# Replacing a bitonic sort of 262,144 edge keys by a fitted network of shrinking gaps, row rotations and a transposed tail

## The chip, the cores and the metric

The kernel runs on one core of a Trainium2 chip. The metric is device time in microseconds of one launch. The engines that matter are TensorE (PE, with its weight loads as PEld), VectorE (DVE), ScalarE (ACT) and GpSimd (POOL); SyncE (SP) issues most DMAs.

## The reference

```python
N, E, D = 4096, 262144, 256
self_out = nodes @ w_self
src_feat = nodes[edges_src]
msg = src_feat @ w_msg
agg = np.zeros((N, D), dtype=np.float32)
np.add.at(agg, edges_dst, msg)
return (self_out + agg).astype(np.float32)
```

Every edge adds one transformed row to its destination. The edges are random, but the draw is the same each time.

## The kernel before

**Products.** The nodes are loaded by POOL's queue with a cast to bf16 (`nodes_bf`), written back to DRAM and read by SP as 64 transposing DMAs into `XT` (L203). TensorE forms `Y = nodes @ w_msg` in 64 products `y_ps` (L213), two for each of 32 blocks of nodes; ScalarE copies them to `Y` (L217).

**Keys.** The edges lie as 128 rows of 2048. Each becomes one whole number below 2^24, held in fp32: the lowest 7 bits are the source within its block of 128 nodes; the rest orders the edges by destination segment (10 segments of 384 nodes and one of 256), then by source block, then by destination. One segment with one source block is a *run*; there are 352.

**Sort.** A bitonic sort of all keys. `cpass` (L574) is one pass: two exchanges on VectorE (L582), a minimum and a maximum over half of the 2048 columns each. 66 passes sort the rows. Then 7 stages join the rows: `_switch` (L554) transposes 16 blocks of 128 x 128 through TensorE (L560) into PSUM, and ScalarE copies them back to SBUF (L563), so that distances between rows become distances between columns. The first and the last pass beside a switch are cut in four (`split=4`), so that a quarter can go on.

**Hand-over.** The sorted keys are cut into 2048 *chunks* of 128. `k16` is each chunk's least key (L225), `gi` that without its 7 low bits, the chunk's base. `gi` goes to DRAM and comes back to all partitions (`gball`, L251, L252), to be subtracted (`rel_b`, L310); small steps turn `gi` into an address in PSUM for each chunk (`poff`), which goes through DRAM into one row (`poffs`, L283).

**Counting and applying.** For every 32 chunks VectorE makes one-hots (L326): `e_oh` of the source in its block (128 wide) and `d_oh` of the destination counted from the chunk's base (W = 96 wide). A matmul for each chunk (L360, `count_mm`) adds e^T d to a ring of 6 PSUM banks, at the address that TensorE loads from `poffs`. Before a run its bank's edges are cleared (L360 too, with `zer`); after it ScalarE evicts the counts to `at` (L386), and TensorE multiplies them with the run's block of `Y` (L410, L415) into `out_ps`; L403 adds the self term at the head of a segment. Six chunks belong to a run (four in the last segment), 192 to a segment. The order of this part is written out by hand, and evictions, clears and applies stand at fixed chunks, so the bases have to lie within margins of the plan.

**Check.** A flag counts the chunks whose base lies outside the margins, or whose span may leave the window. If it isn't zero, `_any_edges` redoes the whole work edge by edge, in 2048 rounds.

The lines that decide how the sort is paced:

```python
for t, op in ((0, ALU.min), (1, ALU.max)):
    nc.vector.tensor_tensor(
        out=d4[:, :, t, :], in0=s4[:, :, 0, :], in1=hi, op=op
    )
```

The functions that the change touches:

Of the kernel before, what the change touches and what calls it, by code (L numbers as in the profile page):

```python
# [9 lines left out]
P = 128  # L10
FP32 = mybir.dt.float32
BF16 = mybir.dt.bfloat16
I32 = mybir.dt.int32
I64 = mybir.dt.int64
# [7 lines left out]
W = 96  # L22
# [6 lines left out]
MARG2 = 6  # L29
LAG = 12  # L30
PSUM0 = 0x2000000
SENT = float((1 << 24) - 1)
# [13 lines left out]
def kernel(  # L46
# [17 lines left out]
    NSTAGE = 18  # L64
    JBITS = 11
# [9 lines left out]
    gd = dram.tile([1, NCOL], FP32, name="gd")  # L75
    pd = dram.tile([1, NCOL], I32, name="pd")
    fd = dram.tile([1, P], FP32, name="fd")
# [9 lines left out]

    sgi = const.tile([P, 8], I32, name="sgi")
    sgx = const.tile([P, 8], I32, name="sgx")
    sgn = const.tile([P, 8], FP32, name="sgn")  # L90
    ksg = const.tile([P, 5], FP32, name="ksg")
    nc.gpsimd.iota(sgi[:], pattern=[[0, 8]], base=0, channel_multiplier=1)
    tss = nc.vector.tensor_single_scalar
    tt = nc.vector.tensor_tensor
    tss(out=sgx[:], in_=sgi[:], scalar=1, op=ALU.logical_shift_right)
    tt(out=sgx[:], in0=sgx[:], in1=sgi[:], op=ALU.bitwise_xor)
    for k in range(7):
        nc.vector.tensor_scalar(
            out=sgx[:, k:k + 1], in0=sgx[:, k:k + 1], scalar1=k, scalar2=1,
            op0=ALU.logical_shift_right, op1=ALU.bitwise_and,  # L100
        )
    tss(out=sgx[:, 7:8], in_=sgi[:, 7:8], scalar=1, op=ALU.bitwise_and)
    nc.vector.tensor_scalar(
        out=sgn[:], in0=sgx[:], scalar1=-2.0, scalar2=1.0, op0=ALU.mult, op1=ALU.add
    )
    for i, m in enumerate((1.0, 128.0, float((SW * (NB - 1)) << 7), float((SW << 7) - P), float(-(1 << 14)))):
        nc.vector.tensor_scalar(
            out=ksg[:, i:i + 1], in0=sgn[:, 7:8], scalar1=m, scalar2=None, op0=ALU.mult
        )

    sortp = tc.alloc_tile_pool(name="sortp", bufs=1)
    XA = [sortp.tile([P, NCOL], FP32, name=f"XA{i}") for i in range(2)]
    XB = [sortp.tile([P, NCOL], FP32, name=f"XB{i}") for i in range(2)]
    sids = [sortp.tile([P, P], FP32, name=f"sid{k}") for k in range(7)]
    for k in range(7):
        nc.gpsimd.tensor_scalar(
            out=sids[k][:], in0=ident[:], scalar1=sgn[:, k:k + 1], scalar2=None, op0=ALU.mult
        )
# [3 lines left out]
    for h in range(2):  # L122
        d64 = ldp.tile([P, HC], I64, name=f"d64_{h}")
        s64 = ldp.tile([P, HC], I64, name=f"s64_{h}")
        nc.sync.dma_start(
            d64[:], edges_dst.rearrange("(p j) -> p j", p=P)[:, h * HC:(h + 1) * HC]
        )
        nc.scalar.dma_start(
            s64[:], edges_src.rearrange("(p j) -> p j", p=P)[:, h * HC:(h + 1) * HC]
        )  # L130
        dlo = d64[:].bitcast(I32)[:, 0::2]
        slo = s64[:].bitcast(I32)[:, 0::2]
        hi = XB[h][:].bitcast(I32)
        seg = hi[:, 0:HC]
        blk = hi[:, HC:2 * HC]
        key = XA[0][:, h * HC:(h + 1) * HC]
        cut = XA[1][:, h * HC:(h + 1) * HC]
        nc.scalar.activation(out=key, in_=slo, func=ACTF.Copy, scale=ksg[:, 0:1])
        tss(out=blk, in_=slo, scalar=7, op=ALU.logical_shift_right)
        tss(out=seg, in_=dlo, scalar=7, op=ALU.logical_shift_right)  # L140
        nc.vector.scalar_tensor_tensor(
            out=cut, in0=seg, scalar=29.5, in1=blk, op0=ALU.is_gt, op1=ALU.mult
        )
        tss(out=seg, in_=seg, scalar=43, op=ALU.mult)
        tss(out=seg, in_=seg, scalar=7, op=ALU.logical_shift_right)
        for v, i in ((dlo, 1), (cut, 4), (seg, 2), (blk, 3)):
            nc.vector.scalar_tensor_tensor(  # L147
                out=key, in0=v, scalar=ksg[:, i:i + 1], in1=key, op0=ALU.mult, op1=ALU.add
            )
# [7 lines left out]
    jrow = const.tile([P, P, 2], BF16, name="jrow")  # L157
    lo_c = const.tile([P, G16], I32, name="lo_c")
    hi_c = const.tile([P, G16], I32, name="hi_c")
    lom_c = const.tile([P, G16], I32, name="lom_c")  # L160

# [58 lines left out]
    lane = _run_sort(nc, psum_sort, XA, XB, ident, sids, NSTAGE, JBITS)  # L220
    srt = XA[0]
    k16 = meta.tile([P, G16], FP32, name="k16")
    for q in range(4):
        _switch(nc, psum_sort, lane, srt, ident, q)
        nc.vector.tensor_reduce(  # L225
            out=k16[:, 4 * q:4 * q + 4],
            in_=_view3(srt[:, q * 512:(q + 1) * 512], P), axis=AX.X, op=ALU.min,
        )


# [5 lines left out]
    gi = meta.tile([P, G16], I32, name="gi")  # L236
    gn = meta.tile([P, G16], I32, name="gn")
# [3 lines left out]
    gb = meta.tile([P, G16], FP32, name="gb")  # L241
# [3 lines left out]
    gball = meta.tile([P, NCOL], FP32, name="gball")  # L245
    poffs = meta.tile([1, NCOL], I32, name="poffs")

    nc.vector.tensor_copy(out=k16i[:], in_=k16[:])
    tss(out=gi[:], in_=k16i[:], scalar=7, op=ALU.logical_shift_right)
    nc.vector.tensor_copy(out=gb[:], in_=gi[:])  # L250
    nc.sync.dma_start(gd[0, :].rearrange("(p g) -> p g", g=G16), gb[:])  # L251
    nc.sync.dma_start(gball[:], gd[0:1, :].broadcast_to([P, NCOL]))  # L252
# [8 lines left out]
    nc.vector.scalar_tensor_tensor(  # L261
        out=dl[:], in0=qa[:], scalar=float(-SW), in1=gi[:], op0=ALU.mult, op1=ALU.add
    )
    nc.vector.scalar_tensor_tensor(
        out=dl[:], in0=qb[:], scalar=-256.0, in1=dl[:], op0=ALU.mult, op1=ALU.add
    )
# [7 lines left out]
    nc.vector.scalar_tensor_tensor(  # L274
        out=wr[:], in0=sl[:], scalar=float(BW), in1=wr[:], op0=ALU.mult, op1=ALU.add
    )
# [9 lines left out]
    SBL = 512  # L286
    ki = meta.tile([P, NCOL], I32, name="ki")
    kl = meta.tile([P, NCOL], I32, name="kl")
    slo_b = meta.tile([P, NCOL], BF16, name="slo_b")
    rel_b = meta.tile([P, NCOL], BF16, name="rel_b")  # L290
    for q in range(NCOL // SBL):
        s = slice(q * SBL, (q + 1) * SBL)
        nc.scalar.copy(  # L293
            out=_view3(ki[:, s], G16),
            in_=lane[:].rearrange("q (g p) -> q p g", g=G16)[:, q * 32:(q + 1) * 32, :],
        )
        tss(out=kl[:, s], in_=ki[:, s], scalar=P - 1, op=ALU.bitwise_and)
        nc.scalar.copy(out=slo_b[:, s], in_=kl[:, s])
        tss(out=ki[:, s], in_=ki[:, s], scalar=7, op=ALU.logical_shift_right)

# [5 lines left out]
    sortp.release()  # L306

    for q in range(NCOL // SBL):
        s = slice(q * SBL, (q + 1) * SBL)
        tt(out=rel_b[:, s], in0=ki[:, s], in1=gball[:, s], op=ALU.subtract)  # L310

# [5 lines left out]

    sizes = [8, 8, 16] + [32] * ((NCOL - 64) // 32) + [16, 8, 8]
    assert sum(sizes) == NCOL

    def onehots(c, n):
        res = []
        for nm, val, wid in (("e", slo_b, P), ("d", rel_b, W)):
# [243 lines left out]

# [62 lines left out]
```

## Time and profile before

| what | value |
|---|---|
| time, median of 3 runs | 783.82 us (783.25 to 785.28) |
| profiled execution | 782.96 us, span 781.1 us |
| VectorE busy | 687.2 us, 88% |
| TensorE busy | 389.3 us, 50% (weight loads 349.5 us beside it) |
| ScalarE busy | 254.5 us, 33% |
| sort on VectorE (L582) | 402.1 us in 490 exchanges |
| one-hots on VectorE (L326) | 259.5 us |

How to read it: rows of a group give line, engine, operation, tile written and tiles read, size, count, then busy time and the mean in ns of one, then the idle time just ahead of them and what ended it. The chain is the work that ended last, followed back from the end: each row has a start, a length and what it is. L numbers in the prediction's rows are those of the kernel before.

### The profile page before, as it was taken

Reading aid. Unit: us, or ns where it says so; the run is one execution under the profiler, and the core shown is the slowest. Engines: PE = TensorE matmul, PEld = TensorE weight load, DVE = VectorE, ACT = ScalarE, POOL = GpSimd, SP = SyncE. Lnnn points to the kernel's source line nnn. Section 1 sums busy time; section 2 is a strip of 40 time slices with the busy share of each in tenths; the row PEclk is TensorE's granted clock in tenths of the full one; section 3 lists DMA queues with packets and bytes.
Section 4 is the critical chain, followed back from the end, with each engine's and each line's share of the span. In section 5 each row is a group of like instructions: output and inputs, shape, how many; then the busy total and the mean of one; then the engine's idle time right before and its main releaser. Section 6 shows DMA issues by size and latency. Waiting matters only on the chain.

```text
span 781.1 us, 10934 instructions
## 1 busy us (share of the span) xinstructions
PE 389.3 (50%) x4351; PEld 349.5 (45%) x4351; DVE 687.2 (88%) x724; ACT 254.5 (33%) x472; POOL 20.4 (3%) x29
## 2 busy tenths in 40 slices
PE   0033330003222233330223302999999999999997
PEld 0000000003222233330222202999989998999986
DVE  4999999998988888889888898999988988898870
ACT  1011110001111111110111104566766766676675
POOL 3400000000000000000000001000000000000000
PEclk9999999999766655555665555899999999999999
DMA  9711110000000000000000001000000000000000
GB/s 285 164 25 26 27 25 0 0 0 1 0 0 0 0 1 0 0 0 0 1 0 0 0 0 58 3 22 18 6 22 22 3 22 22 22 2 22 22 22 17
DMA packets 24939, 16.77 MB, mean 21 GB/s; under 512 B 11444, under 2 KB 24245, under 8 KB 24245
## 3 DMA queue, kind: packets, MB, share of 16 engines
q1 hardware_dynamic: 19796, 11.57, 4.9%
q0 software_dynamic: 4656, 2.36, 2.2%
q10 hardware_dynamic: 434, 2.11, 0.7%
q8 instruction: 36, 0.59, 0.3%
q14 instruction: 17, 0.14, 0.1%
HBM read 9.98 MB, written 6.32 MB: 21 GB/s over the span
## 4 chain that ended last, share of the span: by engine, by line
DVE 47%; PE 45%; ACT 3%; DMA 3%; issue 2%; ACTq 0%; DVEq 0%; SPq 0%
DVE XA L582 30%; PE ring L360 15%; PE out_ps L415 14%; DVE XB L582 14%; PE tp_sw L560 10%; PE out_ps L410 5%; DMA s<-in_edges_src_dram 2%; DVE XA L147 1%; PE out_ps L403 1%; ACT o_sb L424 1%; DMA gball<-gd 1%; ACT XB L563 1%; ACT XA L563 1%; ACT ki L293 0%; DVE rel_b L310 0%
## 5 line engine op out<-in xcount | busy, mean ns | idle before, releaser
L582 DVE TENSOR_TENSOR XA<-XA 128x1024 f32<-128x1024 f32 (+1 forms) x294 | 262.2, 939 | 16.3 <-ACT XA L563 11.7
L386 ACT CAST at<-ring 128x480 bf16<-128x480 f32 (+1 forms) x352 | 193.4, 550 | 96.7 <-PE ring L360 93.3
L326 DVE TENSOR_TENSOR e_oh<-slo_b,jrow 128x4096 bf16<-128x4096 bf16 (+2 forms) x68 | 147.0, 2162 | 27.7 <-PE ring L360 26.9
L415 PE MATMUL out_ps<-Y,at 128*128 128x256 bf16 x1024 | 169.1, 273 | 0.0
L582 DVE TENSOR_TENSOR XB<-XB 128x256 f32<-128x256 f32 (+1 forms) x196 | 139.9, 764 | 19.8 <-ACT XB L563 16.9
L360 PE MATMUL ring<-d_oh,e_oh 128*128 128x96 bf16 x2048 | 148.6, 207 | 10.3 <-DVE e_oh L326 10.3
L360 PEld LDWEIGHTS <-e_oh 128*128 128x128 bf16 x2048 | 124.0, 98 | 14.7 <-issue 9.6
L560 PE MATMUL tp_sw<-sid,XA 128*128 128x128 f32 x224 | 42.1, 374 | 156.9 <-DVE XA L582 156.9
L326 DVE TENSOR_TENSOR d_oh<-rel_b,jrow 128x3072 bf16<-128x3072 bf16 (+2 forms) x68 | 112.5, 1655 | 0.0
L560 PEld LDWEIGHTS tp_sw<-sid,XA 128*128 128x128 f32 x224 | 41.0, 287 | 158.1 <-issue 158.1
L415 PEld LDWEIGHTS <-at 128*128 128x128 bf16 x1024 | 99.4, 97 | 8.3
L560 PE MATMUL tp_sw<-ident,XB 128*128 128x128 f32 x224 | 41.9, 373 | 115.3 <-DVE XB L582 115.3
L410 PE MATMUL out_ps<-Y,at 128*128 128x256 bf16 (+1 forms) x351 | 95.1, 271 | 0.0
L560 PEld LDWEIGHTS tp_sw<-ident,XB 128*128 128x128 f32 x224 | 40.8, 286 | 116.4 <-issue 116.4
L360 PE MATMUL ring<-zer 128*128 128x192 bf16 x352 | 87.1, 248 | 4.0 <-POOL zer L336 4.0
L563 ACT COPY XB<-tp_sw 128x512 f32<-128x512 f32 x28 | 16.4, 586 | 182.8 <-PE tp_sw L560 182.8
L213 PE MATMUL y_ps<-wcat,XT 128*128 128x256 bf16 x64 | 25.3, 395 | 92.4 <-DMA XT<-nodes_bf_dram 92.4
L563 ACT COPY XA<-tp_sw 128x512 f32<-128x512 f32 x28 | 16.3, 587 | 138.1 <-PE tp_sw L560 138.1
L213 PEld LDWEIGHTS <-XT 128*128 128x128 bf16 x64 | 6.7, 104 | 110.7 <-DMA XT<-nodes_bf_dram 110.7
L217 ACT CAST Y<-y_ps 128x256 bf16<-128x256 f32 x32 | 11.9, 372 | 86.5 <-PE y_ps L213 86.5
L360 PEld LDWEIGHTS <-zer 128*128 128x128 bf16 x352 | 34.6, 99 | 8.2 <-POOL zer L336 4.2
L410 PEld LDWEIGHTS <-at 128*128 128x128 bf16 (+1 forms) x351 | 34.5, 98 | 0.2
(83 smaller groups left out, 95.1 us busy)
## 6 DMA issues: line engine op xcount, KB each, us to landing
out_dram<-o_sb SPq DMA_DIRECT2D x11, 256.0 KB, 2.2
s<-in_edges_src_dram ACTq DMA_DIRECT2D x2, 1024.0 KB, 11.1
d<-in_edges_dst_dram SPq DMA_DIRECT2D x2, 1024.0 KB, 10.8
nodes_bf<-in_nodes_dram POOLq DMA_DIRECT2D x1, 2048.0 KB, 21.9
nodes_bf_dram<-nodes_bf SPq DMA_DIRECT2D x1, 2048.0 KB
out_dram<-o_sb SPq DMA_DIRECT2D x10, 128.0 KB, 2.1
XT<-nodes_bf_dram SPq DMA_TRANSPOSE x64, 2.3
gball<-gd SPq DMA_DIRECT2D x1, 1024.0 KB, 4.8
```

Source lines behind the costliest of these rows:

```text
L147: nc.vector.scalar_tensor_tensor(out=key, in0=v, scalar=ksg[:, i:i + 1], in1=key, op0=ALU.mult, op1=ALU.add)
L213: nc.tensor.matmul(out=y_ps[:], lhsT=XT[:, k, t * P:(t + 1) * P], rhs=wcat[:, 2 + k, :], start=(k == 0), stop=(k == 1),)
L217: nc.scalar.copy(out=Y[:, t, :], in_=y_ps[:])
L326: tt(out=o[:, 0:n // 2], in0=val[:, c:c + n].rearrange("p (g i) -> p g i", i=2).unsqueeze(2).to_broadcast(shp), in1=jrow[:, 0:wid, :].unsq ...
L360: mm = nc.tensor.matmul(out=ap, lhsT=lhsT, rhs=rhs, start=start, stop=True, skip_group_check=True,).ins
L386: ins = nc.scalar.copy(out=at[:, 0:n], in_=ring[:, b:b + n]).ins
L403: nc.tensor.matmul(out=out_ps[:, t, :], lhsT=XT[:, k, c0:c0 + P], rhs=wcat[:, k, :], start=(k == 0 and t % 2 == 0), stop=False, skip_group ...
L410: nc.tensor.matmul(out=out_ps[0:m, 0, :], lhsT=at_of.pop(r - 1)[:, w:w + m], rhs=Y[:, b, :], start=False, stop=False, skip_group_check=True,)
L415: nc.tensor.matmul(out=out_ps[:, t, :], lhsT=at[:, t * P:(t + 1) * P], rhs=Y[:, b, :], start=False, stop=(b == NB - 1), skip_group_check=True,
L560: nc.tensor.matmul(out=tp[:, k * P:(k + 1) * P], lhsT=src[:, c], rhs=rhs[:], start=True, stop=True)
L563: nc.scalar.copy(out=dst[:, q * 512:(q + 1) * 512], in_=tp[:])
L582: nc.vector.tensor_tensor(out=d4[:, :, t, :], in0=s4[:, :, 0, :], in1=hi, op=op)
```

## The change

The bitonic sort is replaced by a fixed network with constants of its own. It does not sort fully: it is made so that the 128 keys of a chunk span less than a window, which is widened from 96 to 112.

- `SORT_A` holds 25 *gaps* and 5 *rotations*. A gap m compares column j with column j + m in all rows, first for even blocks of columns, then for odd ones (`gap`). Gaps up to 90 run over pads at the row's ends (a low one of 16 columns, a high one of 128) in four exchanges of 1024 columns; wider ones are cut to the row, into five or seven pieces. The gaps come in the order 859, 1023, 532, 457, 287, 128, 102, 155, 127, 92, rotation, 43, 36, 28, 34, 27, 12, rotation, 12, 10, 5, rotation, 3, rotation, 3, 1, 1, rotation, 1, 3.
- A rotation shifts the rows cyclically by a distance that differs between groups of columns: 16 fp32 products with a shifted identity (`id2`), and 4 copies by ScalarE. Two (`q16`) take 2 columns of every 32, gathered, and write SBUF in pieces of two; three (`q4`) take 4 of every 16 or 2 of every 8 and write PSUM in such pieces.
- Then 32 blocks are transposed, so that 16 columns of all rows become one long row: 2048 columns and a halo of 1024 on either side, which holds copies of the neighbours' keys. Eight gaps from 130 to 16 run on it (`plan`), each over as much halo as the later ones need.
- The base is subtracted from the keys before the last 16 transposes, and ScalarE writes the differences as int16 (`vals`). `gd`, `gball`, `pd`, `poffs` go; TensorE loads its addresses from `poff` in place.
- The source and the distance are split from `vals` in four pieces between the one-hots (`split_vals`), and the one-hots compare int16 in place of bf16.
- The evictions also sum what they copy (`csum`), and the flag is raised too if the sum isn't E. The sum over partitions is a matmul at the end, in place of a round trip through DRAM.
- The signs in the keys, `sids` and their small steps go. The fills of `zer` and `at` stand at the start on POOL.

TensorE's instructions at the end of the products and in the sort. In the kernel before, where sid is the signed identity (rows with x16 are 16 products):

```order
L213 LDWEIGHTS XT
L213 MATMUL y_ps<-wcat,XT 128x256
L560 MATMUL tp_sw<-sid_107,XA_103 128x128 x16
L560 MATMUL tp_sw<-ident,XB_106 128x128 x16
L560 MATMUL tp_sw<-sid_108,XA_104 128x128 x16
L560 MATMUL tp_sw<-ident,XB_106 128x128 x16
```

In the changed kernel, up to the first counting:

```order
L205 LDWEIGHTS XT
L205 MATMUL y_ps<-wcat,XT 128x256
L622 MATMUL tp_sw<-XA_79,id_83 128x128 x16
L622 MATMUL tp_sw<-XA_80,id_83 128x128 x16
L610 MATMUL tp_sw<-XA_80,id_83 128x32x4 x16
L610 MATMUL tp_sw<-XA_80,id_83 128x64x2 x32
L645 MATMUL tp_sw<-id_83,XA_79 128x128 x32
L273 MATMUL tp_sw<-ident,XS_82 128x128 x16
L333 LDWEIGHTS zer
L333 MATMUL ring<-zer 128x2x112
```

In both, all 64 products y_ps stand ahead of the sort's first work on TensorE; the fourteen switches have become five rotations, a transposition of 32 blocks and one of 16.

POOL's queue from the identity to the load of the nodes, before (sgi is for the signs):

```order
masks.py:197 MEMSET ident 128x128
L92 ISA
L92 IOTA sgi 128x8
masks.py:199 AFFINE_SELECT ident<-ident 128x128
L153 MEMSET ones_sent 1x1
L155 DMA wcat<-in_w_self_dram 128x2x256
L156 DMA wcat<-in_w_msg_dram 128x2x256
L164 IOTA jrow_i 128x256
L185 IOTA c_i 128x16
L199 DMA nodes_bf<-in_nodes_dram 128x32x256
```

And in the changed kernel, from the first copy of the identity:

```order
L103 COPY id_83<-ident 128x128 x2
L135 MEMSET ones_sent 1x1
L137 DMA wcat<-in_w_self_dram 128x2x256
L138 DMA wcat<-in_w_msg_dram 128x2x256
L145 MEMSET zer 128x384
...
L152 MEMSET onesc 128x1
L156 IOTA jrow_i 128x256
L177 IOTA c_i 128x16
L191 DMA nodes_bf<-in_nodes_dram 128x32x256
```

The fills of zer and of the six at, the copies of the identity and the pads of XA now precede the load of the nodes.

The core of the diff:

```diff
-W = 96
+W = 112
...
+        scr = XS[h][:].bitcast(I32)
...
-    lane = _run_sort(nc, psum_sort, XA, XB, ident, sids, NSTAGE, JBITS)
+    own = _run_sort(nc, psum_sort, XA, XS, id2, plan, halo)
...
-    nc.sync.dma_start(gd[0, :].rearrange("(p g) -> p g", g=G16), gb[:])
-    nc.sync.dma_start(gball[:], gd[0:1, :].broadcast_to([P, NCOL]))
...
-    nc.scalar.dma_start(pd[0, :].rearrange("(p g) -> p g", g=G16), poff[:])
-    nc.scalar.dma_start(poffs[:], pd[0:1, :])
...
+    for t in range(G16 // 4):
+        tp = psum_sort.tile([P, 512], FP32, name="tp_sw", tag="tp", bufs=4)
+        for k in range(4 * t, 4 * t + 4):
+            s = slice(k * P, (k + 1) * P)
+            nc.vector.tensor_scalar(
+                out=rel[:, s], in0=own[:, s], scalar1=g7f[:, k:k + 1], scalar2=32640.0,
+                op0=ALU.subtract, op1=ALU.min,
+            )
+            nc.tensor.transpose(tp[:, (k % 4) * P:(k % 4 + 1) * P], rel[:, s], ident[:])
         nc.scalar.copy(
+            out=vals[:].rearrange("p (q k) -> p q k", k=G16)[:, :, 4 * t:4 * t + 4],
+            in_=tp[:].rearrange("p (k q) -> p q k", k=4),
+        )
...
-        ins = nc.scalar.copy(out=at[:, 0:n], in_=ring[:, b:b + n]).ins
+        ins = nc.scalar.activation(
+            out=at[:, 0:n], in_=ring[:, b:b + n], func=ACTF.Copy, accum_out=csum[:, r:r + 1],
+        ).ins
...
-                nc.tensor.load(regs, poffs[0:1, c:c + 8])
+                nc.tensor.load(regs, poff[c // G16:c // G16 + 1, c % G16:c % G16 + 8])
...
+    def pair(lo, up, lo_out, up_out):
+        mm(out=lo_out, in0=lo, in1=up, op=ALU.min)
+        mm(out=up_out, in0=lo, in1=up, op=ALU.max)
+
+    def gap(x, y, m):
+        b = m & -m
+        if m <= PADM:
+            n = n_col // (2 * b)
+            for par, u in ((0, x), (1, y)):
+                s = FP + par * b
+                up = _blocks(u, s + m, n, b)
+                pair(_blocks(x, s, n, b), up, _blocks(y, s, n, b), up)
+            return
...
+        elif op[0] == "q4":
+            bb, rots = op[1:]
+            for t in range(4):
+                tp = psum.tile([P, 512], FP32, name="tp_sw", tag="tp", bufs=4)
+                for g in range(4):
+                    r = rots[4 * t + g]
+                    c = FP + 512 * t
+                    sel = lambda v: v.rearrange("p (i g b) -> p i g b", g=4, b=bb)[:, :, g, :]
+                    nc.tensor.matmul(
+                        out=sel(tp[:]), lhsT=id2[:, (P - r) % P:(P - r) % P + P],
+                        rhs=sel(x[:, c:c + 512]), start=True, stop=True,
+                    )
+                nc.scalar.copy(out=y[:, c:c + 512], in_=tp[:])
...
+        for k in range(t, t + w):
+            c = FP + k - halo // P
+            nc.tensor.transpose(
+                tp[:, (k - t) * P:(k - t + 1) * P], x[:, c:c + 16 * (P - 1) + 1:16], id2[:, 0:P]
+            )
+        nc.scalar.copy(out=XS[0][:, t * P:(t + w) * P], in_=tp[:, 0:w * P])
```

More of the change, by code (lines that the diff above doesn't have):

```diff
@@ L13 @@
 I32 = mybir.dt.int32
+I16 = mybir.dt.int16
 I64 = mybir.dt.int64
@@ L305 @@
     ldp.release()
[L306 to L310, printed above, removed]
     psum2 = tc.alloc_tile_pool(name="psum2", bufs=1, space=bass.MemoryType.PSUM)
```

299 lines of the change are left out of this document (159 added, 140 removed).

## The prediction

> **What bounds the kernel now.** First the page: the busy shares, and the chain by line.
>
> ```profile
> PE 389.3 (50%) x4351; PEld 349.5 (45%) x4351; DVE 687.2 (88%) x724; ACT 254.5 (33%) x472; POOL 20.4 (3%) x29
> DVE XA L582 30%; PE ring L360 15%; PE out_ps L415 14%; DVE XB L582 14%; PE tp_sw L560 10%; PE out_ps L410 5%; DMA s<-in_edges_src_dram 2%; DVE XA L147 1%; PE out_ps L403 1%; ACT o_sb L424 1%; DMA gball<-gd 1%; ACT XB L563 1%; ACT XA L563 1%; ACT ki L293 0%; DVE rel_b L310 0%
> ```
>
> There are two stages, one after the other. The chain first runs through the sort on VectorE (L582, 44%) with its switches on TensorE (L560, 10%), then through counting (L360) and applying (L410, L415) on TensorE. Each stage has its own price, so I read the durations by form next, to cost every new instruction by its size.
>
> ```profile
> L582 DVE TENSOR_TENSOR XA<-XA 128x1024 f32<-128x1024 f32 x190 | 224.5, 1222 | 3.6
> L386 ACT CAST at<-ring 128x480 bf16<-128x480 f32 x320 | 179.2, 560 | 91.9 <-PE ring L360 91.8
> L415 PE MATMUL out_ps<-Y,at 128*128 128x256 bf16 x1024 | 169.1, 273 | 0.0
> L360 PE MATMUL ring<-d_oh,e_oh 128*128 128x96 bf16 x2048 | 148.6, 207 | 10.3 <-DVE e_oh L326 10.3
> L326 DVE TENSOR_TENSOR e_oh<-slo_b,jrow 128x4096 bf16<-128x4096 bf16 x62 | 141.8, 2288 | 19.7 <-PE ring L360 19.0
> L326 DVE TENSOR_TENSOR d_oh<-rel_b,jrow 128x3072 bf16<-128x3072 bf16 x62 | 108.4, 1749 | 0.0
> L360 PE MATMUL ring<-zer 128*128 128x192 bf16 x352 | 87.1, 248 | 4.0 <-POOL zer L336 4.0
> L582 DVE TENSOR_TENSOR XA<-XA 128x256 f32<-128x256 f32 x104 | 37.7, 421 | 12.8 <-ACT XA L563 11.7
> L386 ACT CAST at<-ring 128x352 bf16<-128x352 f32 x32 | 14.3, 454 | 4.8 <-PE ring L360 1.5
> L293 ACT CAST ki<-XB 128x512 int32<-128x512 f32 x4 | 4.1, 1085 | 0.0
> L225 DVE TENSOR_REDUCE k<-XA 128x4 f32<-128x512 f32 x4 | 2.6, 682 | 0.5 <-ACT XA L563 0.5
> L310 DVE TENSOR_TENSOR rel_b<-ki,gball 128x512 bf16<-128x512 int32 x4 | 2.5, 686 | 1.0 <-DMA gball<-gd 1.0
> L298 ACT CAST slo_b<-kl 128x512 bf16<-128x512 int32 x4 | 2.4, 636 | 0.5 <-DVE kl L297 0.5
> L138 ACT ACTIVATE XA<-s,ksg 128x1024 f32<-128x1024 int32 x2 | 2.4, 1225 | 6.6 <-DVE ksg L107 6.6
> ```
>
> The chain in order of time gives the pace of the sort, and the start and the period of the counting:
>
> ```profile
> 30.62 1.13 DVE XA L582
> ...
> 43.35 2.37 DVE XA L582 x2
> ...
> 184.71 2.37 DVE XA L582 x2
> ...
> 488.57 2.98 PE ring L360 x31
> ...
> 518.73 0.81 PE out_ps L403 x6
> ...
> 730.69 0.81 PE out_ps L403 x6
> ```
>
> The sort starts at 30.6. Between the next two rows lie 59 passes: 141.36 / 59 = 2.396 us a pass, 1.198 us an exchange of 1024 (24 ns less than its recorded 1222, so neighbours overlap). From 421 and 1222 ns an element costs 801 / 768 = 1.043 ns and an instruction 0.130 us beside it. The six L403 products stand at the head of a segment: 211.96 / 8 = 26.495 us for 192 chunks. Sort and counting meet at 488.57.
>
> **The change: what the first rotation waits for.** A gap m compares 2048 - m pairs, each by a minimum and a maximum; the ten gaps ahead of the rotation add up to 3762, so 2 x (20480 - 3762) = 33,436 elements in 68 instructions (five or seven a gap): 34.9 + 8.8 = 43.7 us. Begun at 30.6, they are over at 74. But in TensorE's order all 64 products y_ps stand ahead of it, and they run at the pace of the transposing loads of XT:
>
> ```profile
> L203 SPq DMA_TRANSPOSE XT<-nodes_bf_dram x64: 1206/1230/1234, 34.6 to 114.9; - x64
> 117.29 0.40 PE L213 MATMUL y_ps<-wcat,XT 128*128 128x256 bf16 x1 [0.81 <-DMA XT<-nodes_bf_dram]
> ```
>
> Before, the first switch came at 188, so this cost nothing. Now VectorE must stand idle from about 74 until 117.7, since the next gap reads what the rotation writes. Whatever the ten first gaps and the shorter key arithmetic save is lost in that wait.
>
> The loads of XT also start later, since the node load has moved back on POOL's queue:
>
> ```profile
> 3.97 1.72 POOL L199 DMA_DIRECT2D nodes_bf<-in_nodes_dram  x1
> 14.74 0.69 DVE L139 TENSOR_SCALAR XB<-s 128x1024 int32<-128x1024 int32 x1 [2.00 <-DMA s<-in_edges_src_dram]
> 25.88 0.42 SPq L200 DMA_DIRECT2D nodes_bf_dram<-nodes_bf  x1
> L340 POOL MEMSET at<- 128x512 bf16 x6 | 3.3, 586 | 0.0
> L116 POOL TENSOR_SCALAR sid<-ident,sgn 128x128 f32<-128x128 f32 x7 | 10.3, 1483 | 11.1 <-DVE sgn L103 11.1
> ```
>
> Six fills of at (3.3), zer and the smaller fills (1.2) and two copies of the identity (at most 1.48 each) now precede it: up to 7.5 us late. Against that, the edge loads occupy the DMA engines until 14.74 in either case, and then leave it more room: 0 at the other end. I take 3. The y products end at 120.7.
>
> **Rotations.** A switch of 16 fp32 products, which is what a rotation is:
>
> ```profile
> 188.01 6.22 PE L560 MATMUL tp_sw<-sid,XA 128*128 128x128 f32 x32 [70.33 <-DVE XA L582]
> ...
> 193.38 0.59 ACT L563 COPY XB<-tp_sw 128x512 f32<-128x512 f32 x1 [0.99 <-PE tp_sw L560]
> 194.00 11.65 DVE L582 TENSOR_TENSOR XB<-XB 128x256 f32<-128x256 f32 x18 [0.81 <-ACT XB L563]
> 194.27 0.59 ACT L563 COPY XB<-tp_sw 128x512 f32<-128x512 f32 x1 [0.31 <-PE tp_sw L560]
> ```
>
> Before, passes cut in four let VectorE start on a quarter (194.00, before the last copy). The gaps aren't cut, so each rotation stands bare: 6.2 + 0.6 + 0.1 = 6.9 us. The last quarter of a switch follows the one before by 0.89 us, the pace of a warmed-up TensorE. The two q16 rotations write SBUF in pieces of two; the nearest row is the copy that reads SBUF across a stride, 1085 ns against 636 in a row, so 7.4.
>
> - Rotation 1: 120.7 + 7.4 = 128.1.
> - Fifteen gaps of at most 43, four exchanges of 1024 each: 60 x 1.198 = 71.9, to 200.0.
> - Four more rotations, 7.4 + 3 x 6.9 = 28.1: 228.1.
> - 32 transposes with halo: at the switch's pace 6.2 + 4 x 0.89 = 9.8. Their stationary operand is read at every sixteenth element; by the strided copy's ratio (1085 / 636 = 1.7) 16.6. A strided SBUF read is what that row shows, so I take 16.6, plus 0.7 for the last copy: 245.4. Ends: 9.8 and 20.
> - Tail: 32 exchanges, four a gap, from 1864 and 1734 elements at gap 130 to 1056 and 1040 at gap 16 (each twice), 41,716 in all: 43.5 + 4.2 = 47.7, to 293.1. The halo makes these 27% longer than 2048-wide passes (32 x 1024 elements) would be.
> - Chunk minimum: 682 + 1536 x 1.043 = 2.3 us, and three small dependent steps, 0.6: 296.0.
> - Sixteen subtractions with 21 small steps between them run beside 16 transposes on TensorE: 0.2 + 6.2 + a strided copy 1.1: 303.5. The removed work (two round trips through DRAM, four ki copies, four rel_b) lay here, 470 to 488.
> - Splitting 64 columns 0.35, the first e_oh 0.7, the first read of poff into registers, which now comes after that e_oh on TensorE: between nothing and 2.5, taken 1.5. Counting starts at 306.0 in place of 488.6: **182.6 us less**.
>
> On the strided reads and writes the Trainium skill (SBUF — State Buffer, Door 1: The DMA port swizzle) says that SBUF is read in lines of 16 bytes, with a penalty for each access to another line, and that any non-contiguous pattern in PSUM, whose lines have 8 bytes, slows matmuls significantly. For the transposes this is the strided copy's side, 16.6. For the three q4 rotations, which write PSUM in pieces of two or four floats, it speaks against my 6.9; no row here has such a write, since the clear L360 jumps only once.
>
> **Counting with windows of 112.** From the three product rows, (273 - 207) / 160 = 0.41 ns a column. Added are 2048 x 16 + 352 x 32 = 44,032 columns: 18.1 us. Upper end: the stage's mean, 26.495 us / 58,880 columns of a segment = 0.45, 19.8 us. Lower end from this stretch:
>
> ```profile
> 494.14 0.36 PEld L360 LDWEIGHTS <-e_oh 128*128 128x128 bf16 x6
> 494.22 0.42 PE L360 MATMUL ring<-d_oh,e_oh 128*128 128x96 bf16 x6
> DVE e_oh L326 <- PE ring L360: 26.9, 24, 4.4
> ```
>
> The loads follow each other at (0.36 - 0.098) / 5 = 52 ns, the products at 43. If the loads set the pace the counting products grow for nothing, and only the clears cost: 4.6. With six loads against eleven products a run they don't, so 18.1. VectorE: d_oh grows by 512 x 0.526 = 0.27 us, a pair is 4.31 and six pairs 25.8 a segment, under TensorE's 28.2; it waited 26.9 us for TensorE before, and still waits.
>
> ScalarE: an eviction of 496 costs 573 ns by the two CAST rows (0.828 ns a column). It is now an ACTIVATE that also sums. The only ACTIVATE row has 1225 - 848 = 377 ns beside its elements, the CAST 163. Ends: 0.57, and 0.57 + 0.21 + one more instruction of 0.16 = 0.95. A run lasts 28.2 / 32 = 0.88, less 0.03 for o_sb: hidden up to 0.85. I take 0.76.
>
> At the end the flag now depends on the last eviction, a product behind the last apply and four small steps, beside the last output copy and DMA:
>
> ```profile
> 774.89 0.38 PE L415 MATMUL out_ps<-Y,at 128*128 128x256 bf16 x2
> 775.92 0.38 SPq L425 DMA_DIRECT2D out_dram<-o_sb  x1
> out_dram<-o_sb SPq DMA_DIRECT2D x11, 256.0 KB, 2.2
> ```
>
> Some 2 us of check beside 3.2 us of output, then the register reads: 0 to 2.5, taken 1.0.
>
> **Sum.** The profiled execution took 782.96 (span 781.1 and 1.9 around it; the median of runs is 783.82): 782.96 - 182.6 + 18.1 + 1.0 = 619.5, said as **620**.
>
> **Rivals.**
> - ScalarE becomes the bound of counting, if an eviction takes over 0.85 us. At 0.95: 352 x 0.95 - 3.4 + 10.4 = 341 in place of 305, so 656; at 0.90, 638. The 91.8 us that it waited for TensorE speak against it, the one ACTIVATE row for it. 12%.
> - The pieces in PSUM slow the q4 rotations, the row's 6.2 doubled: +18.7, 638. It is the skill's rule above made into a time. 8%.
> - All lower ends together: contiguous-speed transposes (-6.8), no delay of the nodes (-3), counting products grown for nothing (-13.5): 597. 5%.
> - Slower: one-hots from int16 lose VectorE's doubled rate. The row L310, with a 32-bit input, costs (686 - 154) / 512 = 1.04 ns an element against 0.526. A pair would take 8.3 us, 64 of them 532, and VectorE would bound the stage: 620 + 227 = 847. The gain is gone from 7.3 us a pair on, where the stage reaches 305 + 164 us. For it: nothing in the trace compares int16; against it: width, not type, separates the fast from the slow rows. 4%.
> - The change doesn't do what it says: the network isn't a full sort, and if a chunk spans 112 blocks or more the total misses E and the edge-by-edge loop runs too. Its 2048 rounds have three dependent DMAs each; at the shortest row, 1.4 us,
>
> ```profile
> kd<-k SPq DMA_DIRECT2D x1, 8.0 KB, 1.4
> ```
>
> that is 8,600 us more. Carrying the exchanges out on the drawn edges gives a widest span of 109, so 1%.
>
> **How the numbers follow.** The forecast itself has 70%, with its own range 604 to 636 from the ends of its terms. To hold 8 in 10 I go down to 600 and up to 648, which takes in the PSUM rival and half of ScalarE's. Faster by over 0.3% (about what a measurement here can tell from no change): 70 + 12 + 8 + 5 = 95%. Slower: 4 + 1 = 5%, half a point of which goes to no change.
>
> **What would show it.** In the changed profile: VectorE idle some 43 us from 74 on, released by a copy behind y_ps, and 5 rotations of 7 us idle each; L645 at 16 us over 32 products (10 would move the sum by -7); the exchanges of 1024 still at 1.2 us; counting from 306 on, with segments of 28.2 us; at evictions under 0.85 us with ScalarE waiting for TensorE. The prediction is wrong if segments are longer than 29 us, if d_oh of 3584 takes near 4 us, or if the first rotation starts before 117.

## The result, and the profile after

Before, the median is 783.84 us (783.25 to 785.28); changed, it is **608.58 us** (607.44 to 609.76). The ratio is 0.776, with a 95% interval of 0.7744 to 0.778. Predicted were 620 and a range of 600 to 648. The profiled execution took 608.38 us, with a span of 606.5.

The page of the changed kernel, busy shares and the chain that ended last, cut by line:

```profile
PE 365.0 (60%) x4113; PEld 324.4 (53%) x4113; DVE 461.1 (76%) x388; ACT 274.4 (45%) x792; POOL 9.7 (2%) x28
PE 51%; DVE 22%; SPq 13%; DMA 5%; ACT 5%; issue 2%; POOL 1%; ACTq 0%; DVEq 0%; POOLq 0%
```

VectorE was busy for 687.2 us and now is for 461.1. Its share of the chain, of which the sort (L582) alone held 44%, is now 22% in all, and SP's DMA queue, which was not among the lines of the chain before, holds 13%: that is the transposing load of XT, on which the first rotation waits. The turning points, from the answers in order of time (start, duration, engine, line; in brackets the idle time ahead and what ended it):

```profile
26.35 0.77 DVE L581 TENSOR_TENSOR XA<-XA 128x595 f32<-128x595 f32 x1
...
117.59 0.40 PE L205 MATMUL y_ps<-wcat,XT 128*128 128x256 bf16 x1 [0.86 <-DMA XT<-nodes_bf_dram]
117.78 5.71 PE L622 MATMUL tp_sw<-XA,id 128*128 128x128 f32 x32
...
123.53 0.59 ACT L626 COPY XA<-tp_sw 128x512 f32<-128x512 f32 x1 [0.30 <-PE tp_sw L622]
124.15 1.23 DVE L562 TENSOR_TENSOR XA<-XA 128x1024 f32<-128x1024 f32 x1 [55.00 <-ACT XA L626]
125.41 1.23 DVE L563 TENSOR_TENSOR XA<-XA 128x1024 f32<-128x1024 f32 x1
126.67 1.23 DVE L562 TENSOR_TENSOR XA<-XA,XA 128x1024 f32<-128x1024 f32 x1
...
226.86 5.78 PE L645 MATMUL tp_sw<-id,XA 128*128 128x128 f32 x32 [10.91 <-DVE XA L563]
...
233.42 2.10 DVE L562 TENSOR_TENSOR XS<-XS 128x1864 f32<-128x1864 f32 x1 [6.70 <-ACT XS L648]
...
283.05 2.29 DVE L237 TENSOR_REDUCE k<-XS 128x16 f32<-128x2048 f32 x1
...
293.65 0.44 PE L333 MATMUL ring<-d_oh,e_oh 128*128 128x112 bf16 x3 [1.28 <-DVE d_oh L305]
```

The rows show, in this order: the wide gaps from 26.35 on, the last product y_ps with rotation 1 right behind it, the 55.00 us for which VectorE stood idle until then, the first exchanges behind the rotation, the halo transposes (32 records, 6.70 us in which VectorE waits), the tail from 233.42 to 283.05, and the first counting product at 293.65. Before, that one stood at 488.57.

The counting: the heads of two segments in the chain in order of time, then the page's groups (busy us, mean ns of one, idle time ahead), and one group of VectorE by form:

```profile
327.63 0.81 PE out_ps L378 x6
...
554.41 0.82 PE out_ps L378 x6
```

```profile
L333 PE MATMUL ring<-d_oh,e_oh 128*128 128x112 bf16 x2048 | 164.0, 214 | 2.7 <-DVE d_oh L305 2.7
L359 ACT ACTIVATE at<-ring 128x496 bf16<-128x496 f32 (+1 forms) x352 | 202.0, 574 | 69.7 <-PE ring L333 68.2
L359 ACT ACTIVATION_READ_ACCUMULATOR at<-ring 128x1 f32 x352 | 68.7, 195 | 0.0
```

```profile
L305 DVE TENSOR_TENSOR d_oh<-rel_b,jrow 128x3584 bf16<-128x3584 int16 x62 | 125.1, 2017 | 0.0
```

A full segment is (554.41 - 327.63) / 8 = 28.35 us in place of 26.495. TensorE still sets its pace there: ScalarE waits 68.2 us for it and VectorE 27.4. An eviction is two instructions now, 574 and 195 ns.

So 194.9 us came out ahead of the counting and 20.3 went back: from 488.57 to the end it was 292.5 us, from 293.65 it is 312.85.

### The profile page after: what moved, and what is told of

Read it like the earlier page. It is cut to its first block, busy times and chain, and to the rows that moved or that the text cites. A ratio compares the mean times of both kernels' runs of the same rounds, so it can differ in the third digit from the quotient of the medians.

```text
span 606.5 us, 10333 instructions
## 1 busy us (share of the span) xinstructions
PE 365.0 (60%) x4113; PEld 324.4 (53%) x4113; DVE 461.1 (76%) x388; ACT 274.4 (45%) x792; POOL 9.7 (2%) x28
## 4 chain that ended last, share of the span: by engine, by line
PE 51%; DVE 22%; SPq 13%; DMA 5%; ACT 5%; issue 2%; POOL 1%; ACTq 0%; DVEq 0%; POOLq 0%
PE ring L333 21%; PE out_ps L390 17%; SPq L195 13%; DVE XA L562 6%; DVE XA L563 6%; PE out_ps L385 6%; DVE XS L563 4%; DVE XS L562 4%; ACT at L359 3%; PE tp_sw L610 3%; DMA nodes_bf<-in_nodes_dram 3%; PE tp_sw L622 2%; DMA nodes_bf_dram<-nodes_bf 2%; PE out_ps L378 1%; ACT o_sb L399 1%
## 5 line engine op out<-in xcount | busy, mean ns | idle before, releaser
L359 ACT ACTIVATE at<-ring 128x496 bf16<-128x496 f32 (+1 forms) x352 | 202.0, 574 | 69.7 <-PE ring L333 68.2
L305 DVE TENSOR_TENSOR e_oh<-slo_b,jrow 128x4096 bf16<-128x4096 int16 (+2 forms) x68 | 147.1, 2164 | 28.8 <-PE ring L333 27.4
L333 PE MATMUL ring<-d_oh,e_oh 128*128 128x112 bf16 x2048 | 164.0, 214 | 2.7 <-DVE d_oh L305 2.7
L333 PEld LDWEIGHTS <-e_oh 128*128 128x128 bf16 x2048 | 138.4, 98 | 6.6 <-issue 2.5
L305 DVE TENSOR_TENSOR d_oh<-rel_b,jrow 128x3584 bf16<-128x3584 int16 (+2 forms) x68 | 129.7, 1907 | 0.0
L333 PE MATMUL ring<-zer 128*128 128x224 bf16 x352 | 91.8, 261 | 0.7 <-ACT vals L274 0.7
L562 DVE TENSOR_TENSOR XA<-XA 128x1024 f32<-128x1024 f32 x15 | 18.4, 1226 | 82.4 <-ACT XA L626 62.0
L359 ACT ACTIVATION_READ_ACCUMULATOR at<-ring 128x1 f32 x352 | 68.7, 195 | 0.0
L610 PE MATMUL tp_sw<-XA,id 128*128 128x128 f32 x96 | 17.6, 365 | 37.7 <-DVE XA L563 37.7
L610 PEld LDWEIGHTS tp_sw<-XA,id 128*128 128x128 f32 x96 | 17.1, 278 | 38.2 <-issue 38.2
L622 PE MATMUL tp_sw<-XA,id 128*128 128x128 f32 x64 | 11.9, 367 | 31.0 <-DVE XA L563 31.0
## 6 DMA issues: line engine op xcount, KB each, us to landing
nodes_bf<-in_nodes_dram POOLq DMA_DIRECT2D x1, 2048.0 KB, 17.6
```

The costliest lines, as they stand in the source:

```text
L305: tt(out=o[:, 0:n // 2], in0=val[:, c:c + n].rearrange("p (g i) -> p g i", i=2).unsqueeze(2).to_broadcast(shp), in1=jrow[:, 0:wid, :].unsq ...
L333: mm = nc.tensor.matmul(out=ap, lhsT=lhsT, rhs=rhs, start=start, stop=True, skip_group_check=True,).ins
L359: ins = nc.scalar.activation(out=at[:, 0:n], in_=ring[:, b:b + n], func=ACTF.Copy, accum_out=csum[:, r:r + 1],).ins
L562: mm(out=lo_out, in0=lo, in1=up, op=ALU.min)
L610: nc.tensor.matmul(out=sel(tp[:]), lhsT=id2[:, (P - r) % P:(P - r) % P + P], rhs=sel(x[:, c:c + 512]), start=True, stop=True,)
L622: nc.tensor.matmul(out=tp[:, g * P:(g + 1) * P], lhsT=id2[:, (P - r) % P:(P - r) % P + P], rhs=sel(x)[:, 4 * t + g], start=True, stop=True,)
```

## The experiments

**1. What the wait for XT costs.** The 64 products y_ps and their copies are issued behind the last halo transpose:

```
-    for t in range(T):
-        y_ps = ...                       # ahead of the sort
     own, last_tp = _run_sort(...)
+    with tc.issue_after(last_tp):
+        for t in range(T):
+            y_ps = ...
```

> The 64 products y_ps stand behind the 32 halo transposes in TensorE's order instead of ahead of the first rotation; nothing else is changed. Theory (the first rotation waits only for its place behind the products, which wait for XT): VectorE ends the ten wide gaps at 69.1 and goes on after one bare rotation of 6.2 at 75.3 in place of 124.15, so 48.9 us less, about 560 us; the products then run beside the tail on VectorE, where TensorE and ScalarE are idle for 50 us. Rival A (the products only move the wait: 64 products and 32 copies do not fit beside the tail and hold up the last 16 transposes): 560 plus 10 to 25, so 570 to 585. Rival B (the rotations are slow or late as long as the transposing loads run, whatever the order): little change, 600 or more.

Measured: 561.12 us (559.07 to 561.35), ratio 0.7162 (0.7149 to 0.7174). In order of time:

```profile
69.38 5.32 PE L623 MATMUL tp_sw<-XA,id 128*128 128x128 f32 x32 [69.38 <-DVE XA L593]
...
75.35 1.23 DVE L563 TENSOR_TENSOR XA<-XA 128x1024 f32<-128x1024 f32 x1 [6.12 <-ACT XA L627]
```

The rotation follows the last wide gap at once, VectorE goes on at 75.35 in place of 124.15 (48.8 us), and the segment that began at 327.63 starts 49.3 us earlier (278.30). The y products run beside the tail (their last copies at 196.55) and cost nothing: from VectorE's return to the first segment's head it is 202.95 us, 203.48 in the changed kernel. So of the 55.00 us of idle time, 48.9 were the place of the products and their copies ahead of the rotation, and 6.12 are the rotation itself. That wait is worth 47.5 us of the changed kernel's time; both rivals fell.

**2. The later node load.** It is issued first on POOL's queue, ahead of the weights and the fills:

```
+    nc.gpsimd.dma_start(nodes_bf[:], nodes...)   # ahead of the fills of zer and at
     zer = const.tile([P, 3, P] ...
```

> On POOL's queue the load of the nodes stands ahead of the weights and of the fills of zer and at, so it is issued at about 2.2 us in place of 7.67. Theory (the load shares the DMA engines with the 4 MB of edges and lands when all bytes are through, near 25 us, whatever its place in the queue): XT's loads begin at 34 to 35 as now, no change, 607 to 609. Rival (the queue position sets the landing, and the chain of the first 118 us begins on POOL): up to 5.5 us less, 603.

Measured: 607.8 us (605.23 to 608.45), ratio 0.7746 (0.773 to 0.7763). The load's issue and the issue of what reads it, in the changed kernel and then here:

```profile
7.67 1.72 POOL L191 DMA_DIRECT2D nodes_bf<-in_nodes_dram  x1
25.30 0.43 SPq L192 DMA_DIRECT2D nodes_bf_dram<-nodes_bf  x1
34.84 6.31 SPq L195 DMA_TRANSPOSE XT<-nodes_bf_dram  x5
```

```profile
2.15 1.82 POOL L149 DMA_DIRECT2D nodes_bf<-in_nodes_dram  x1
24.36 0.43 SPq L192 DMA_DIRECT2D nodes_bf_dram<-nodes_bf  x1
33.35 7.58 SPq L195 DMA_TRANSPOSE XT<-nodes_bf_dram  x6
```

Issued 5.5 us earlier, the load lands 0.9 us earlier: it takes 22.2 us in place of 17.6. While the edge loads are on their way, little of it moves: from 14 to 24 us, with the edges in, the DMA engines move 196 to 199 GB/s in either kernel, which comes to 2.0 MB, nearly the whole load. The first load of XT moves by 1.5 us, within the scatter of that start over the kernels run here (33.1 to 35.1 in their profiles). The place in POOL's queue is worth nothing that can be told from no change.

**3. The windows of 112 by themselves.** The kernel before, with one number changed:

```
-W = 96
+W = 112
```

> The kernel before with windows of 112 in place of 96 and nothing else changed. Theory (TensorE streams the counting's columns, 0.41 to 0.45 ns each): 44,032 more columns, 18 to 20 us more, 802 to 804 us, and segments of 28.2 to 28.4 us in place of 26.5. Rival (the weight loads of 52 ns set the pace of the counting products): only the clears grow, 4.6 us, 788 to 789.

Measured: 801.77 us (800.62 to 802.7), ratio 1.0229 (1.0209 to 1.025), 18.3 us more than the 783.47 that the kernel before took beside it. From the chain:

```profile
521.77 0.81 PE out_ps L403 x6
...
747.66 0.81 PE out_ps L403 x6
```

(747.66 - 521.77) / 8 = 28.24 us a segment, 1.74 more. Nearly all that the counting gave back is the width of the windows, priced by columns.

**4. The totals.** Evictions as plain copies; the total of the counts is left out of the flag:

```
-        ins = nc.scalar.activation(out=at[:, 0:n], in_=ring[:, b:b + n], func=ACTF.Copy, accum_out=csum[:, r:r + 1]).ins
+        ins = nc.scalar.copy(out=at[:, 0:n], in_=ring[:, b:b + n]).ins
```

> The changed kernel with the evictions as plain copies, without the sums (the total is left out of the flag). Theory (the sums, 0.195 us an eviction, lie in ScalarE's slack, since an eviction with its sum takes 0.78 of the 0.886 us that a run lasts): no change in the segments of 28.35 us; at most 1 us less at the end, where the flag waited for the last sum, so 607 to 608.5. Rival (ScalarE paces the last 32 runs, which last 0.625 us each, as long as an eviction and its sum there): those runs fall to about 0.60, 1 us or a little more less in addition, 606. If ScalarE paced all of the counting: 600 or less.

Measured: 605.08 us (604.45 to 607.08), ratio 0.773 (0.7715 to 0.7744). VectorE's return from rotation 1 in order of time, and the heads of two segments of the chain:

```profile
121.92 1.23 DVE L559 TENSOR_TENSOR XA<-XA 128x1024 f32<-128x1024 f32 x1 [52.62 <-ACT XA L623]
```

```profile
324.71 0.81 PE out_ps L375 x6
...
550.63 0.81 PE out_ps L375 x6
```

That is 3.5 us less than the changed kernel, more than either side expected, but little of it is the sum's: a segment takes 28.24 us in place of 28.35, 1.1 us over ten of them. In its profile 2.2 us were ahead already when VectorE came back from rotation 1 (121.92), in a stretch that the edit does not touch: 1.6 because the loads of XT begin at 33.24 in place of 34.84, within the scatter told in 2, and 0.6 because rotation 1 is that much shorter. The rival on the last 32 runs fell: from the head of the last segment to the last product of applying it is 18.5 us in both (582.99 to 601.50, and 579.07 to 597.58), although in the changed kernel the chain runs through the evictions there. ScalarE gets 35.5 us of waiting back (it waits 103.7 us for TensorE in place of 68.2) and the time hardly moves: the second instruction of an eviction is hidden but for 0.11 us a segment.

**5. Single prices, measured in idle stretches.** The changed kernel with extra instructions in two places: on VectorE in the idle time ahead of rotation 1, on TensorE behind the halo transposes.

```
+    for i in range(4):                                     # A (L631, L632)
+        mm(out=ev[3], in0=ev[0], in1=od[0], op=ALU.min)
+        mm(out=od[4], in0=ev[0], in1=od[0], op=ALU.max)
+    for i in range(4):                                     # B (L634, L635)
+        mm(out=od[1], in0=ev[0], in1=od[1], op=ALU.max)
+        mm(out=od[2], in0=ev[0], in1=od[2], op=ALU.max)
+    for i in range(4):                                     # C (L637, L638)
+        mm(out=ev[3], in0=ev[0], in1=od[1 + i % 2], op=ALU.min)
+        mm(out=od[1 + i % 2], in0=ev[0], in1=od[1 + i % 2], op=ALU.max)
+    for i in range(4):                                     # D (L640, L641)
+        mm(out=ev[3], in0=ev[4], in1=od[0], op=ALU.min)
+        mm(out=ev[4], in0=ev[3], in1=od[0], op=ALU.max)
...
+    # behind the halo transposes, 32 each: transposes (L685) of x[:, c:c + 2033:16], of x[:, c:c + 128];
+    # then matmul(lhsT=..., rhs=id2[:, 0:P]) (L687) of the one and of the other
```

> The changed kernel with two rows of extra instructions, put where the engine is idle, so that single prices can be read from the trace (the result is not touched). On VectorE, in the 55 us ahead of the first rotation's return, 32 exchanges of 1024 on scratch data: eight whose neighbours have nothing in common (A), eight in place whose neighbours have nothing in common (B), eight as the changed kernel has them, a minimum and then a maximum in place on what the minimum has just read (C), eight of which each reads what the one ahead has just written, none in place (D). On TensorE, behind the 32 halo transposes, 32 more of the same, 32 with the stationary operand in a row, 32 fp32 products against the identity with the strided operand, 32 with the operand in a row. Theory for VectorE: it is the tie to the neighbour that costs: A and B 1.13 us from start to start, D 1.26, C 1.26 from minimum to maximum and 1.13 on. Rival: writing in place costs: A and D 1.13, B and C 1.26. Theory for TensorE: a transpose is one pass and an fp32 product two, and the stride costs nothing: both groups of transposes 6 to 7 us, both groups of products 9 to 13. Rival, as I had priced it: the stride costs a factor of 1.7 in both forms. Time of the kernel 608 to 610.

Measured: 608.06 us, one run. VectorE first, in order of time; then TensorE in four stretches, laid close to where the form of the instructions changes (length, busy time, records, granted clock, DMA):

```profile
74.42 1.22 DVE L631 TENSOR_TENSOR XS<-SB 128x1024 f32<-128x1024 f32 x1
75.56 1.22 DVE L632 TENSOR_TENSOR XS<-SB 128x1024 f32<-128x1024 f32 x1
...
83.50 1.22 DVE L634 TENSOR_TENSOR XS<-SB,XS 128x1024 f32<-128x1024 f32 x1
84.64 1.22 DVE L635 TENSOR_TENSOR XS<-SB,XS 128x1024 f32<-128x1024 f32 x1
...
92.58 1.23 DVE L637 TENSOR_TENSOR XS<-SB,XS 128x1024 f32<-128x1024 f32 x1
93.84 1.23 DVE L638 TENSOR_TENSOR XS<-SB,XS 128x1024 f32<-128x1024 f32 x1
94.98 1.22 DVE L637 TENSOR_TENSOR XS<-SB,XS 128x1024 f32<-128x1024 f32 x1
...
102.17 1.22 DVE L640 TENSOR_TENSOR XS<-XS,SB 128x1024 f32<-128x1024 f32 x1
103.43 1.23 DVE L641 TENSOR_TENSOR XS<-XS,SB 128x1024 f32<-128x1024 f32 x1
```

```profile
231.90:235.55 3.65, 3.65 (x33) 1.00 0.00 0
235.55:239.00 3.45, 3.45 (x34) 1.00 0.00 0
239.00:252.30 13.30, 13.30 (x63) 1.00 0.00 1
252.30:260.40 8.10, 7.99 (x68) 1.00 0.00 0
```

All rows have the same recorded duration, 1.22 us; only the starts tell the price. Free neighbours (A) and in-place free ones (B) start 1.14 us apart. In C the maximum, which overwrites what the minimum just read, starts 1.26 behind it, and the next, free, minimum 1.14 behind that. In D each step is 1.26; but D's exchanges do both at once, they read what the one ahead wrote and overwrite what it read. A read behind a write by itself stands in the changed kernel: the minimum of a gap's second half (126.67) reads what the maximum ahead of it wrote, overwrites nothing that it read, and starts 1.26 behind it too. So the tie to the neighbour costs 0.12 us, of either kind and of both together, and writing in place costs nothing: theory, not rival.

On TensorE a transpose is one record, and the records start 0.11 us apart, strided or not: 3.6 us for 32 where the theory had 6 to 7, since all of them ran at the full granted clock. The products are two records. In the windows a record on an edge counts on both sides, and the third ends a few records before the form changes; by their starts, the 64 records with the strided operand stand 0.22 us apart, the 64 with the operand in a row 0.11. Here both were half right: the stride is free for the transpose, and costs the product a factor of 2.0.

**6. The tie taken away from every second exchange.** In the gaps up to 90 and in the tail, the maximum goes to a third tile Z (the gaps' part; starts and counts are left out, and the tail has the same):

```
-            for par, u in ((0, x), (1, y)):
-                ...
-                pair(_blocks(x, s, n, b), up, _blocks(y, s, n, b), up)
+            for par, w, u, lo_to, up_to in ((0, x, x, y, Z), (1, Z, y, x, x)):
+                ...
+                pair(_blocks(w, s, n, b), _blocks(u, s + m, n, b), _blocks(lo_to, s, n, b), _blocks(up_to, s + m, n, b))
```

> The exchanges of the gaps up to 90 and of the tail write their maximum to a third tile instead of in place, and the second half of a gap brings both back to the first tile; the same pairs, 8 elements more an exchange on average. The result stays the same. Theory (an exchange tied to the one ahead costs 1.26 us, a free one 1.13): every second exchange is now free of its neighbour, as before the change: 1.198 us in the mean, 92 exchanges x 0.062 = 5.7 us less, less 0.6 for the added elements: 603 to 604. Rival, that writing in place costs by itself: all of them 1.135, 11.5 us less, 597. Rival, that the row of exchanges has that pace anyhow: 608 to 609.

Measured: 601.26 us (600.16 to 602.48), ratio 0.7671 (0.766 to 0.7682). In order of time:

```profile
123.01 1.25 DVE L564 TENSOR_TENSOR XA<-XA 128x1045 f32<-128x1045 f32 x1 [53.80 <-ACT XA L632]
124.17 1.24 DVE L565 TENSOR_TENSOR Z<-XA 128x1045 f32<-128x1045 f32 x1
125.45 1.25 DVE L564 TENSOR_TENSOR XA<-Z,XA 128x1046 f32<-128x1046 f32 x1
...
229.04 2.10 DVE L564 TENSOR_TENSOR XS<-XS 128x1864 f32<-128x1864 f32 x1 [7.12 <-ACT XS L654]
...
276.70 2.29 DVE L239 TENSOR_REDUCE k<-XS 128x16 f32<-128x2048 f32 x1
```

Steps of 1.16 and 1.28 now alternate. From rotation 1's return to the tail it is 106.0 us (109.3 before the edit), and the tail is 47.7 (49.6): 5.2 us, as the tie has it, where 5.1 were expected. The profiled executions differ by 5.9 us (608.38 and 602.48): beside the 5.2, 1.1 lie ahead of 123.01 (the loads of XT begin at 33.11 in place of 34.84, and rotation 1 is longer by 0.7), and 0.4 are lost behind the tail. The medians differ by 7.3 us, more than the theory had; where the other 1.4 lie is not shown. The rival on writing in place fell by the steps.

**7. The halo transposes as products:**

```
-            nc.tensor.transpose(tp[...], x[:, c:c + 16 * (P - 1) + 1:16], id2[:, 0:P])
+            nc.tensor.matmul(out=tp[...], lhsT=x[:, c:c + 16 * (P - 1) + 1:16], rhs=id2[:, 0:P], start=True, stop=True)
```

> The 32 halo transposes are written as fp32 products of the same strided operand against the identity, which move the same data. Theory: a product is two passes where a transpose is one, and the stride is free: the stage takes the 9.8 us that I had as its lower end in place of 6.7, the kernel 611 to 612. Rival: the stride of sixteen costs for products as I had priced it, 16.6 us: 618. Rival: copies set the pace of the stage, no change: 608 to 609.

Measured: 616.04 us (615.43 to 616.98), ratio 0.7867 (0.7855 to 0.788). In order of time:

```profile
225.98 14.21 PE L645 MATMUL tp_sw<-id,XA 128*128 128x128 f32 x64 [10.91 <-DVE XA L563]
...
240.85 2.10 DVE L562 TENSOR_TENSOR XS<-XS 128x1864 f32<-128x1864 f32 x1 [15.01 <-ACT XS L649]
```

15.01 us of waiting in place of 6.70, 7.5 us in the time. The theory's 9.8 fell, and the rival's 16.6 came close: what I had priced was this kernel. In three stretches (length, then busy time and records of TensorE first, the granted clock behind the engines):

```profile
225.90:230.00 4.10, 4.02 (x18) 4.05 (x19) 0.00 (x0) 0.74 (x2) 0.00 (x0) 0.50 0.00 0
230.00:235.00 5.00, 5.00 (x25) 5.00 (x24) 0.00 (x0) 1.61 (x4) 0.00 (x0) 0.98 0.00 0
235.00:240.30 5.30, 5.19 (x24) 5.00 (x23) 0.00 (x0) 1.82 (x4) 0.00 (x0) 1.00 0.00 0
```

The strided products gain nothing from the clock: by their starts the records stand 0.22 us apart at 0.50 as at 1.00. So the 0.22 of experiment 5 is no slow clock either: there the transposes just ahead of the products ran at 0.11.

**8. Experiments 1 and 6 together** (both edits as above).

> Both edits together: the y products behind the halo transposes (561.1 alone) and the third tile. Theory: with the wait for XT gone the sort is VectorE's alone, so the 5 us of the third tile come off in full: 555 to 557. Rival, the third tile gives nothing: 560 to 561.

Measured: **555.62 us** (555.17 to 556.63), ratio 0.7097 (0.7085 to 0.7108), against 561.12 with the first edit alone. It is the fastest of the kernels here. Its chain by engine:

```profile
PE 56%; DVE 33%; ACT 5%; DMA 2%; issue 2%; ACTq 0%; DVEq 0%
```

Expected were 555 to 557. SP's queue has left the chain; it now runs through VectorE and TensorE as before, with about half the time ahead of the counting (240.41 us in place of 488.57).

## Why the prediction was right, and where it was off

It held because its one large point held: the first rotation waits for the y products in TensorE's queue, and their pace is that of the transposing loads. Predicted were an idle VectorE from 74 to 128.1, measured 69.15 to 124.15, and taking that wait away gave 47.5 us. What the forecast had wrong ahead of the wait, an end of the wide gaps that came 5 us earlier, could cost nothing, since the wait took it up. The steps, in us (durations, in the prediction's order):

| step | predicted | measured | off |
|---|---|---|---|
| last y product over | at 120.7 | at 118.0 | -2.7 |
| rotation 1 | 7.4 | 6.2 | -1.2 |
| 60 exchanges of 1024 | 71.9 | 75.5 | +3.6 |
| rotations 2 to 5 | 28.1 | 27.1 | -1.0 |
| 32 halo transposes | 17.3 | 6.7 | **-10.6** |
| tail, 32 exchanges | 47.7 | 49.6 | +1.9 |
| chunk minimum and steps | 2.9 | 2.9 | 0 |
| subtractions and transposes | 7.5 | 5.8 | -1.7 |
| split to first product | 2.5 | 1.8 | -0.7 |
| counting starts | at 306.0 | at 293.65 | -12.35 |
| from there to the end | 311.6 | 312.85 | +1.2 |

Together 11.1 us, the whole distance of 619.5 to the profiled 608.38. Errors of both signs stand in it: without the exchanges and the tail, which came out 5.5 us longer, it would be 16.6.

- **The halo transposes are the mis-sized term.** The mechanism, a stage of TensorE alone between two stages of VectorE, was right; the price was not. It came from a row of products (L560, two records each) and was multiplied by a copy's stride ratio. A transpose is one record, and the stride does not touch it (experiment 5); the same stage as products took 15.0 (experiment 7), near the 17.3. That it came so near is luck: the 1.7 was measured on ScalarE, while for these products the stride costs a factor of 2.0 at the full granted clock and hardly anything at half of it (0.22 against 0.21). That the own lower end was 9.8 shows the same slip: it too was a product's price. The Trainium skill (Perfetto Trace Analysis, Transposes) asks for transposes to be written as such, not as a standard matmul; here that is 7.5 us.
- **Exchanges.** The step that took 1.198 us from the passes before was off by 5%: before, minimum and maximum of a pass were free of each other, so only every second exchange was tied to its neighbour (1.198 is near the mean of 1.14 and 1.26, experiment 5). The change writes the maximum in place, and all are tied: 1.26. With every second one freed again, the tail took the predicted 47.7 (experiment 6). The pace of a pass should have been read as two prices, and the new code for which of them it pays.
- **The nodes' delay** was taken as 3, between 0 and 7.5; the last y product starts at 117.59 in place of 117.29, so it was next to 0, the lower end, for the reason given with that end: the edge loads fill the DMA engines meanwhile (experiment 2).
- **Strides of the rotations.** ScalarE's copy that writes SBUF in pieces of two took 0.59 us, not the 1085 ns taken from a row that reads across a stride, and the products that write PSUM in pieces of two and four show no surcharge, by VectorE's waits (total, times, longest; the 62.0 holds rotation 1's 55.0):

```profile
DVE XA L562 <- ACT XA L626: 62.0, 2, 55.0
DVE XA L562 <- ACT XA L614: 20.1, 3, 7.4
```

The three q4 rotations cost 20.1 us, 6.7 each, beside the 6.9 priced from a switch in a row. The rule of the Trainium skill (SBUF — State Buffer, Door 1: The DMA port swizzle) that non-contiguous PSUM patterns slow matmuls significantly is not borne out by these writes, and that rival (638) fell: at the full clock the records start 0.11 to 0.12 us apart whether they write in a row or in pieces. Pieces of one float were not tried. What the Trainium skill says in the same place of SBUF, a penalty for each access to another line of 16 bytes, agrees with the products of experiment 5, whose operand is read at a stride of sixteen floats (0.22 against 0.11), and not with the transposes.
- **Counting.** 18.1 us for the columns: the segments say 28.35 against the 28.2 forecast, and experiment 3 gives 18.3 for the width alone. The lower end, products that grow for nothing, fell: 207 became 214 ns a record, and the pace followed the columns.
- **ScalarE** takes 574 + 195 = 769 ns an eviction in the mean over both widths, where 0.76 was taken and 0.85 would have decided; it waited 68.2 us, so its rival fell. int16 one-hots kept their rate: d_oh of 3584 takes 2.0 us. The check at the end cost none of the 1.0: from the start of the last products of applying to the end of the span it is 5.0 us (601.50 to 606.5), and it was 6.2 before (774.89 to 781.1).

## What to carry to other kernels

When a change shortens a stage, look at what stands ahead of its next instruction in the queue of every engine that it needs: work that once had 70 us of room (here the y products, over at 117.7 where the first switch came at 188) becomes the wait, and moving it behind the stage gave another 8% of the changed kernel's time. Price an instruction from a row of the same instruction; a transpose is no product, and a ratio borrowed from another engine is a guess. Read the pace of a row of VectorE instructions from their starts, apart for tied and free neighbours, since the recorded durations are the same.

## What the runs showed of the hardware

- VectorE overlaps free neighbours of 1024 fp32 elements (1.14 us from start to start) and not tied ones (1.26); overwriting what the instruction ahead reads is a tie like reading what it wrote.
- A 128x128 fp32 transpose took 0.11 us at the full granted clock, with its data at a stride of sixteen as well as in a row; the fp32 product took twice 0.11 in a row and twice 0.22 at that stride, and twice 0.22 at half the clock too (experiment 7). Why product and transpose differ was not tried.
- The halo transposes begin at half the granted clock, after 11 us without work for TensorE, and end at the full one (0.90 in the mean of the second stretch):

```profile
226.00:230.50 4.50, 3.64 (x17) 3.67 (x18) 0.71 (x1) 1.75 (x3) 0.00 (x0) 0.50 0.00 0
230.50:233.50 3.00, 2.14 (x17) 1.95 (x15) 0.08 (x1) 2.64 (x5) 0.00 (x0) 0.90 0.00 0
```

Busy time and records of TensorE are the first pair, the granted clock stands behind the engines: 17 records in 3.64 us, then 17 in 2.14. At experiment 5's pace the stage's 32 would have taken about 3.6 us (an estimate). Every rotation goes through the same two paces: its records begin 0.21 us apart and end 0.11 apart, and the 32 of them last 5.4 to 6.6 us in the changed kernel, according to when the change comes. In rotations 2 to 5 the granted clock goes from 0.50 to 1.00 with it. In rotation 1 it reads 1.00 from the start, and the pace changes all the same (14 records in the 2.80 us to 120.50, then 21 in 2.99), so there the granted clock does not tell the pace; why is open.
